# Gate and up products of a feed-forward layer: one weight sum made by an accumulating transfer, casts and loads in a new order, fifth and sixth product wide in 17 blocks

## The chip, the cores and the metric

The kernel runs on one core of one Trainium2 chip. The metric is the device time of one execution in microseconds (us). A core has TensorE (PE in the profile; PEld are its weight loads), VectorE (DVE), ScalarE (ACT), GpSimd (POOL) and SyncE (SP). SP and POOL issue the transfers of this kernel; 16 DMA engines of the core carry them all.

## The reference

One decoder layer over 512 tokens of width 1024 in float32: a mixer (stick-breaking attention beside a gated short convolution), a cross-attention into 256 memory tokens, and a SwiGLU feed-forward block, each with an RMS norm ahead and a residual add behind. The change lies in the first half of the feed-forward block:

```python
hf = rms_norm(x, norm_ffn[l])
gate, up = jnp.split(hf @ w_ffn_in[l], 2, axis=-1)      # 1024 x (2 * 2816)
x = x + (jax.nn.silu(gate) * up) @ w_ffn_out[l]
```

## The kernel before, in words

**Blocks and products.** The 2816 hidden channels are worked off in 22 blocks of 128 (`NF`, block number `m`). For one block the weights form a 2 x 2 scheme (gate or up, even or odd 128-row part of the 1024 inputs), and so do the activations (tokens 0 to 255 or 256 to 511, even or odd part). The kernel uses the seven-product form of a 2 x 2 matrix product: products `i` = 0 to 6, each of 128 channels by 256 tokens, summed over `KP` = 4 pairs of parts. "Fifth and sixth product" are `i` = 4 and 5. Products 0, 3, 4 and 5 go to the PSUM bank `z` of the block, 1 to `v`, 2 and 6 to `y` ("zvyzzzy"). Products 3, 4 and 5 are added onto what stands in `z`, so ACT or DVE read `z` between them; likewise product 6 is added onto product 2 in `y`.

**High and low parts.** Every operand is split into a rounded high part (float32r, cast by ACT) and a low part (the difference, by DVE). A product is high times high, high times low and low times high. *Narrow*, this is three matmuls of 256 columns for each k, twelve in all. *Wide*, the two halves of the activation lie side by side, so one matmul of 512 columns does the first two terms into the two halves of the bank, and one of 256 columns does the third: eight in all. A wide product leaves a second half in the bank that must be added. Before the change products 1, 2 and 6 are wide in all blocks, 5 in the 14 blocks of `WIDE` (5 to 18), and 0, 3 and 4 in none.

**Weight forms.** `ffn_load(m)` fetches for each block: `wg` (two parts as they are: products 0 and 1), and `ws`, one part loaded twice by SP, onto which POOL issues an accumulating transfer of two further parts (products 4 and 2). `sum_third` (DVE) adds a part of `ws` onto the first half of `wg`: product 3. `load_corner` fetches one more part into the tile `w2` (rows `a`; product 5), and `sum_last` (DVE) writes the sum of the two halves of `wg` beside it: product 6. Each pair is then cast by ACT and its low part taken by DVE: cast A (`pair_cast(m, 0)`, from `wg`), B (`pair_cast(m, 1)`, from `ws`), C (`pair_cast(m, 2)`, from the corner tile), and T (`third_cast(m)`, one half). "Rest A" and so on below are the DVE subtractions behind these casts (`rest_of`; line 1006 in the profile).

**What sets the order.** PE, ACT and DVE run an order written out by hand: the list `uses` names products in turn, in the middle of the stage (m,3), (m,2), (m,4), (m+1,0), (m+1,1), (m,5), (m,6) and so on; behind each product stands what reads it (`reads`), and then what `at` and `made` hang on that place (`made` puts the cast there and the rest one or two places later). Here and below (m,i) is product i of block m. SP and POOL are ordered by the framework: a transfer waits for its own data and for its buffer, and for what stands ahead of it in its queue. `wr` has four buffers and `wg` of `fpool` two: together the `ws` and `wg` of three blocks.

**Evictions.** `second(m)` joins product 2 in `y` with what ACT copied out of `z` after product 4; `evict(m, 0..2)` scales, applies SiLU (ACT) and multiplies; in `WIDE` blocks `evict(m, 2)` first adds the two halves of `z`.

Of the kernel before, what the change touches and what calls it, by code (L numbers as in the profile page):

```python
# [8 lines left out]
F32 = mybir.dt.float32  # L9
F32R = mybir.dt.float32r  # L10
AF = mybir.ActivationFunctionType
ALU = mybir.AluOpType
# [32 lines left out]
def hybrid_layer(ctx: ExitStack, tc: tile.TileContext, xT_d, memT_d, mem_d, cols_d, wv_d, win_d,  # L45
# [18 lines left out]
    def nm(s):  # L64
        count[0] += 1
        return f"{s}{count[0]}"
# [40 lines left out]
    def after(i, earlier):  # L107
        for e in earlier:
            tc.add_manual_dep(i.ins, e.ins.name, mybir.DependencyInfo(
                mybir.DependencyClass.NoSync, mybir.DependencyReason.DATA), reason="order")  # L110
# [588 lines left out]
    def forms_of(xe, xo):  # L699

        b11, b12, b21, b22 = xe[:, :HS], xe[:, HS:], xo[:, :HS], xo[:, HS:]
        c, d = f(unit("c1")), f(unit("c2"))
        n1, t3, n2, t4 = c[:, :HS], c[:, HS:], d[:, :HS], d[:, HS:]
        nc.vector.tensor_tensor(out=n1, in0=b11, in1=b12, op=ALU.subtract)
        nc.vector.tensor_tensor(out=t3, in0=b22, in1=b12, op=ALU.subtract)
        nc.vector.scalar_tensor_tensor(out=n2, in0=n1, scalar=-1.0, in1=b22, op0=ALU.mult,  # L708
                                       op1=ALU.subtract)
        nc.vector.scalar_tensor_tensor(out=t4, in0=n2, scalar=-1.0, in1=b21, op0=ALU.mult,  # L710
                                       op1=ALU.subtract)
        u = unit("xf")
        nc.scalar.copy(u[:, :HS], b11)
        nc.vector.tensor_tensor(out=u[:, HS:], in0=b11, in1=f(u[:, :HS]), op=ALU.subtract)
        a, b = slice(0, HS), slice(HS, S)

        def beside(src, s):
            both = unit(s)
            nc.scalar.copy(both[:, a], src)
            nc.vector.tensor_tensor(out=both[:, b], in0=src, in1=f(both[:, a]), op=ALU.subtract)  # L720
            return both[:, a], both[:, b], both

        first = beside(b21, "xo")
        second, fourth = beside(n1, "xc"), beside(t3, "xc")
        third, fifth = beside(n2, "xd"), beside(t4, "xd")
        last = beside(b22, "xo")
        return [(u[:, a], u[:, b]), first, second, third[:2], fourth[:2], fifth, last]

    def residual(w_dram, act, old, gain, pairs=False):

# [112 lines left out]

    KP = KD // 2
    raws, corners = {}, {}

    def ffn_load(m):

        a = wfi_d[m].rearrange("p (i c) -> p i c", i=4)
        s13, wg = ((fpool, "wg") if (m % 3, t) in ((1, "ws"), (2, "wg")) else (wpool, "wr")  # L850
                   for t in ("ws", "wg"))
        s13 = s13[0].tile([P, 2, 512], F32, tag=s13[1], name=nm("ws"))
        i = nc.sync.dma_start(s13, a[:, 2:3, :].broadcast_to([P, 2, 512]))
        if m < 2:
            after(i, [loads[-6]])
        wg = wg[0].tile([P, 2, 512], F32, tag=wg[1], name=nm("wg"))
        i = nc.sync.dma_start(wg, a[:, 0:2, :])
        if m < 2:
            after(i, [loads[-6]])
        if m < 2:  # L860
            load_corner(m)
        nc.gpsimd.dma_start(s13, a[:, 0:4:3, :], accum_op=ALU.add)  # L862
        raws[m] = wg, s13

    def load_corner(m):

        a22 = corners[m] = fpool.tile([P, 2, 512], F32, tag="w2", name=nm("a22"))
        i = nc.sync.dma_start(a22[:, 0, :], wfi_d[m][:, 3 * 512:])
        if m < 2:
            after(i, [loads[-6]])  # L870
# [4 lines left out]

    def sum_last(m, eng=nc.vector):
        wg = raws[m][0]
        eng.tensor_tensor(out=corners[m][:, 1, :], in0=wg[:, 0, :], in1=wg[:, 1, :], op=ALU.add)

    wforms = {}  # L880

    def pair_cast(m, which):

        raw = (*raws[m], corners[m])[which]
        hi = wpool.tile([P, 2, 512], F32R, tag="wh", name=nm("wf"))
        lo = wpool.tile([P, 2, 512], F32R, tag="wl", name=nm("wf"))
        nc.scalar.copy(hi, raw)
        for n, i in enumerate(((0, 1), (4, 2), (5, 6))[which]):
            wforms[m, i] = hi[:, n, :], lo[:, n, :]
        return raw, hi, lo  # L890
# [11 lines left out]
    def product(ps, m, i, ks=range(KP)):  # L902

        rests = []
        for k in ks:
            hi, lo = (w[:, k * P:(k + 1) * P] for w in wforms[m, i])
            xh, xl, *both = x2f[k][i]
            if both and (i != 5 or m in WIDE):
                nc.tensor.matmul(ps, hi, both[0], start=i < 3 and k == 0, stop=False,  # L909
                                 skip_group_check=True)  # L910
                rests.append((ps[:, :HS], lo, xh))
                continue
            for j, (a, b) in enumerate(((hi, xh), (hi, xl), (lo, xh))):
                nc.tensor.matmul(ps[:, :HS], a, b, start=i < 3 and k == 0 and j == 0,  # L914
                                 stop=k == KP - 1 and j == 2, skip_group_check=True)
        for operands in rests:
            nc.tensor.matmul(*operands, start=False,  # L917
                             stop=ks[-1] == KP - 1 and operands is rests[-1],
                             skip_group_check=True)

    WIDE = range(5, NF - 3)
    banks, silus = {}, []
    acts = {}

# [10 lines left out]
    def joined_halves(out_, bank, old):  # L935
        nc.vector.tensor_tensor(out=out_, in0=bank[:, :HS], in1=old, op=ALU.add)
        nc.vector.tensor_tensor(out=out_, in0=bank[:, HS:], in1=out_, op=ALU.add)

    def reads(m, i):

        b = banks[m]
        z, s, t = b["z"][:, :HS], b["s"], b["t"]
        if i == 5 and m in WIDE:
            nc.scalar.copy(s[:, :HS], b["z"][:, HS:])
        elif i in (0, 3, 4):
            nc.scalar.copy((s[:, :HS], None, None, s[:, HS:], t[:, :HS])[i], z)  # L946
        elif i == 1:
            joined_halves(b["g"][:, :HS], b["v"], s[:, :HS])
        elif i == 6:
            joined_halves(b["g"][:, HS:], b["y"], s[:, HS:])  # L950

    def second(m):
        b = banks[m]
        joined_halves(b["t"][:, HS:], b["y"], b["t"][:, :HS])

    def evict(m, part):
        b = banks[m]
        g = b["g"]
        if part == 0:
            nc.vector.tensor_tensor(out=g, in0=g, in1=r2b[0], op=ALU.mult)  # L960
        elif part == 1:
            silus.append(nc.scalar.activation(g, g, AF.Silu))
        else:
            j, odd = divmod(m, 2)
            if not odd:
                acts[j] = f(unit("a1")), f(unit("a2"))
            to = slice(odd * HS, (odd + 1) * HS)
            first = b["z"][:, :HS]
            if m in WIDE:
                first = b["s"][:, :HS]  # L970
                nc.vector.tensor_tensor(out=first, in0=b["z"][:, :HS], in1=first, op=ALU.add)
            for half, u in enumerate((first, b["t"][:, HS:])):
                sl = slice(half * HS, (half + 1) * HS)
                nc.vector.scalar_tensor_tensor(out=acts[j][half][:, to], in0=u, scalar=-1.0,
                                               in1=g[:, sl], op0=ALU.mult, op1=ALU.mult)
            if not odd:
                n1 = acts[j][1][:, :HS]
                nc.vector.tensor_tensor(out=n1, in0=acts[j][0][:, :HS], in1=n1, op=ALU.subtract)
# [140 lines left out]
    def at(n, *some):  # L1119
        todo.setdefault(n, []).extend(some)  # L1120
# [16 lines left out]
    at(14, lambda: evict(0, 1))  # L1137
    at(15, lambda: evict(0, 2))
    for m in range(NF - 2):
        at(uses.index((m, 1)), lambda m=m: ffn_load(m + 2))  # L1140
    for m in range(1, NF - 1):
        p = {i: uses.index((m, i)) for i in range(2, 7)}
        q = {i: uses.index((m + 1, i)) for i in range(2)}
        if m > 1:
            at(p[3], lambda m=m: sum_third(m + 1))
            at(p[3], lambda m=m: evict(m - 1, 0))
            at(p[2], lambda m=m: evict(m - 1, 1))
            at(q[0], lambda m=m: evict(m - 1, 2))
            made(p[3], pair_cast, m, 2)
            made(p[2], third_cast, m + 1)  # L1150
        else:
            made(p[4], third_cast, m + 1)
        at(p[4], lambda m=m: second(m))
        if m + 2 < NF:
            at(p[4], lambda m=m: load_corner(m + 2))
        made(q[0], pair_cast, m + 1, 1, late=2)
        at(q[1] if m < NF - 2 else p[4], lambda m=m: sum_last(m + 1))
        if m + 2 < NF:
            made(p[5], pair_cast, m + 2, 0)
    at(uses.index((0, 4)), lambda: second(0))  # L1160

# [373 lines left out]
```

## Time and profile before

| | |
|---|---|
| three runs | 839.65 us median (839.28 to 840.1) |
| the profiled execution | 838.75 us, of it a span of 837.0 us |
| granted TensorE clock | 0.998 |
| busy in the span | PE 828.8 us, DVE 684.6, ACT 463.9, POOL 161.2 |
| gate and up stage | from about 502.5 to 721.3 us of the span |
| in it, busy | PE 218.82 us of 218.82, DVE 210.82, ACT 121.81, POOL 24.83 |

The profile gives the span in microseconds from its start. A row of the chain or of the timeline starts with its start and its length; the length of a matmul in the timeline is its latency, so that neighbours overlap, and the time that a product takes is the distance from its start to the next one's. A group's row ends with its busy time, the mean length of one in ns, and the idle time of the engine just before its members. "x12" counts instructions.

### The profile page before, as it was taken

To read this page: it belongs to the slowest core of one execution; us is meant where nothing else is said; L and a number is where in the kernel's file an instruction comes from. 1 tells how busy PE (TensorE), PEld (TensorE's weight loads), DVE (VectorE), ACT (ScalarE), POOL (GpSimd) and SP (SyncE) were. 2 spreads that over 40 slices of the span, in tenths; PEclk is the share of its full clock that TensorE was granted. 3 is DMA by queue.
4 is the path that set the end of the run, shared out by engine and by line. 5 is a ranking of instruction groups with operands and counts; after the bars stand their busy time and mean duration, and the time that the engine had idled before them with its cause. 6 is when DMAs were issued, how large, how long until landed. Compare 5 with 4: busy or idle time off the path is not lost.

```text
span 837.0 us, 11962 instructions
## 1 busy us (share of the span) xinstructions
PE 828.8 (99%) x4374; PEld 714.1 (85%) x4374; DVE 684.6 (82%) x1086; ACT 463.9 (55%) x796; POOL 161.2 (19%) x168
## 2 busy tenths in 40 slices
PE   9999999999999999999999999999999999999996
PEld 7888888888888888888888789999999999888885
DVE  7879899996756576587555698999999999999886
ACT  7567868674332355434444566645555555576654
POOL 0011131110566630173000031111111110000401
PEclk9999999999999999999999999999999999999999
DMA  8552435235687865566431326677767673465552
GB/s 303 155 166 101 122 111 103 74 115 174 228 312 276 304 249 188 182 233 249 148 82 51 101 51 161 167 184 200 197 180 197 176 184 95 170 213 197 180 183 101
DMA packets 51357, 143.69 MB, mean 172 GB/s; under 512 B 5761, under 2 KB 7041, under 8 KB 48482
## 3 DMA queue, kind: packets, MB, share of 16 engines
q1 hardware_dynamic: 41650, 107.89, 38.2%
q0 software_dynamic: 9360, 34.75, 15.8%
q8 instruction: 34, 0.56, 0.3%
q10 hardware_dynamic: 288, 0.28, 0.1%
q14 instruction: 25, 0.20, 0.1%
HBM read 125.20 MB, written 13.64 MB: 166 GB/s over the span
## 4 chain that ended last, share of the span: by engine, by line
PE 99%; DVE 0%; ACT 0%; DVEq 0%; issue 0%
PE z L914 13%; PE p L1228 12%; PE pr L161 8%; PE pr L162 8%; PE pr L163 8%; PE y L909 5%; PE r L162 3%; PE r L163 3%; PE r L161 3%; PE v L288 3%; PE y L917 2%; PE v L909 2%; PE km L666 2%; PE mq L163 2%; PE mq L161 2%; PE mq L162 2%
## 5 line engine op out<-in xcount | busy, mean ns | idle before, releaser
L156 ACT CAST wh<-wr 128x1024 fp32r<-128x1024 f32 x84 | 88.0, 1051 | 144.2 <-issue 80.0
L157 DVE TENSOR_TENSOR wl<-wr,wh 128x1024 fp32r<-128x1024 f32 x84 | 111.0, 1321 | 32.0 <-ACT wh L156 31.9
L161 PE MATMUL pr<-xgh,wh 128*128 128x512 f32 x288 | 112.8, 392 | 0.0
L162 PE MATMUL pr<-xgl,wh 128*128 128x512 f32 x288 | 112.4, 390 | 0.0
L163 PE MATMUL pr<-xgh,wl 128*128 128x512 f32 x288 | 112.3, 390 | 0.0
L611 POOL TENSOR_TENSOR pre<-pre 128x512 f32<-128x512 f32 x44 | 70.9, 1616 | 31.5 <-DMA pre<-in_w_ffn_out_dram 29.2
L862 POOL DMA_DIRECT2D ws<-in_w_ffn_in_dram x22 | 26.6, 1209 | 248.5 <-DVE c L708 54.0
L163 PEld LDWEIGHTS pr<-xgh,wl 128*128 128x128 f32 x288 | 54.1, 188 | 11.5
L161 PEld LDWEIGHTS pr<-xgh,wh 128*128 128x128 f32 x288 | 54.1, 188 | 10.6
L162 PEld LDWEIGHTS pr<-xgl,wh 128*128 128x128 f32 x288 | 54.1, 188 | 10.5
L914 PE MATMUL z<-xd,wf 128*128 128x256 f32 x360 | 47.5, 282 | 0.0
L946 ACT COPY sa<-z 128x256 f32<-128x256 f32 x44 | 16.4, 373 | 51.9 <-PE z L914 51.9
L914 PEld LDWEIGHTS z<-xd,wf 128*128 128x128 f32 x360 | 45.0, 190 | 0.1
L1006 DVE TENSOR_TENSOR wf<-wg,wf 128x1024 fp32r<-128x1024 f32 (+1 forms) x44 | 43.1, 978 | 1.5
L1006 DVE TENSOR_TENSOR wl<-wr,wh 128x1024 fp32r<-128x1024 f32 x33 | 41.0, 1242 | 1.8 <-ACT wh L1073 1.8
L1073 ACT CAST wh<-wr 128x1024 fp32r<-128x1024 f32 x33 | 34.5, 1050 | 5.3 <-ACT f01h L1002 2.6
L914 PE MATMUL z<-xf,wf 128*128 128x256 f32 x264 | 35.4, 283 | 0.0
L914 PE MATMUL z<-xc,wf 128*128 128x256 f32 x264 | 35.1, 283 | 0.0
L914 PEld LDWEIGHTS z<-xf,wf 128*128 128x128 f32 x264 | 33.4, 192 | 0.1
L914 PEld LDWEIGHTS z<-xc,wf 128*128 128x128 f32 x264 | 33.0, 190 | 0.0
L368 DVE TENSOR_TENSOR g<-pr,r0b 128x512 f32<-128x512 f32 x16 | 11.0, 687 | 23.5 <-PE pr L163 23.5
L417 POOL TENSOR_SCALAR_AFFINE_SELECT e<-e 128x128 f32<-128x128 f32 (+1 forms) x24 | 10.7, 447 | 86.6 <-DVE e L470 86.6
(356 smaller groups left out, 2239.9 us busy)
## 6 DMA issues: line engine op xcount, KB each, us to landing
wr<-in_w_in_dram SPq DMA_DIRECT2D x36, 512.0 KB, 3.4
pre<-in_w_ffn_out_dram POOLq DMA_DIRECT2D x11, 1024.0 KB, 8.0
sums<-pre POOLq DMA_DIRECT2D x11, 1024.0 KB, 5.0
ws<-in_w_ffn_in_dram SPq DMA_DIRECT2D x22, 512.0 KB, 4.8
wg<-in_w_ffn_in_dram SPq DMA_DIRECT2D x22, 512.0 KB, 4.7
ws<-in_w_ffn_in_dram POOLq DMA_DIRECT2D x22, 512.0 KB, 5.7
wr<-sums SPq DMA_DIRECT2D x22, 512.0 KB, 4.0
wr<-in_w_ffn_out_dram SPq DMA_DIRECT2D x16, 512.0 KB, 3.7
```

What stands on the lines that cost most here:

```text
L156: after(nc.scalar.copy(h2, raw), lead[-1:])
L157: lows.append(nc.vector.tensor_tensor(out=l2, in0=raw, in1=f(h2), op=ALU.subtract))
L161: nc.tensor.matmul(ps, a[0], b[0], start=start, stop=False, **kw)
L162: nc.tensor.matmul(ps, a[0], b[1], start=False, stop=False, **kw)
L163: nc.tensor.matmul(ps, a[1], b[0], start=False, stop=stop, **kw)
L611: nc.gpsimd.tensor_tensor(out=t[:, a, :], in0=t[:, a, :], in1=t[:, b, :], op=ALU.add)
L862: nc.gpsimd.dma_start(s13, a[:, 0:4:3, :], accum_op=ALU.add)
L909: nc.tensor.matmul(ps, hi, both[0], start=i < 3 and k == 0, stop=False, skip_group_check=True)
L914: nc.tensor.matmul(ps[:, :HS], a, b, start=i < 3 and k == 0 and j == 0, stop=k == KP - 1 and j == 2, skip_group_check=True)
L1006: nc.vector.tensor_tensor(out=lo, in0=src, in1=f(hi), op=ALU.subtract)
L1073: nc.scalar.copy(hi, raw)
L1228: nc.tensor.matmul(res[i][s2], a[:, ts], b, start=j == 0 and n == 0, stop=n == 2 and j == (BEHIND - 1 if (i, s2) == (5, 1) else NJ - 1))
```

## The change

1. Product 4 becomes wide in the blocks of `WIDE`, as product 5 already is, and `WIDE` becomes blocks 3 to 19 (17 blocks, before 5 to 18). So 17 products 4 and three products 5 (blocks 3, 4, 19) become wide. In these blocks ACT copies both halves of `z` after product 4 (512 columns, before 256), and `second` becomes `folded`: one DVE add of 512 columns, one of 256 (before two of 256).
2. In blocks 4 to 20 (`OWN`) `sum_last` is no DVE add: POOL issues a transfer that accumulates the first half of `wg` onto its second half, within SBUF. The corner part is then loaded over the first half of `wg`, and cast C reads `wg`. The tile `w2` is left for blocks 0 to 3 and 21.
3. For these blocks the order changes: `ws` is loaded earlier in the program than `wg` from block 6 on, cast A stands one product earlier, `sum_third` stands directly behind rest A (two products earlier), cast T one product earlier ahead of cast C, and the corner load three products later by the program.

DVE, from rest C of block 7 on (the low part of its corner pair). Before:

```order
L1006 TENSOR_TENSOR wf1139_5661<-a221108_5464,wf1138_5660 128x1024
L1006 TENSOR_TENSOR wf1141_5674<-wg1119_5504,wf1141_5674 128x512
L936 TENSOR_TENSOR sb1129_5583<-y1140_5663,sb1129_5583 128x256
L937 TENSOR_TENSOR sb1129_5583<-y1140_5663,sb1129_5583 128x256
L971 TENSOR_TENSOR sa1110_5467<-z1109_5466,sa1110_5467 128x256
L974 SCALAR_TENSOR_TENSOR a11146_5710<-sa1110_5467,fg1117_5491 128x256
L974 SCALAR_TENSOR_TENSOR a21147_5711<-sb1111_5468,fg1117_5491 128x256
L978 TENSOR_TENSOR a21147_5711<-a11146_5710,a21147_5711 128x256
L936 TENSOR_TENSOR fg1151_5720<-v1150_5719,sa1144_5695 128x256
L937 TENSOR_TENSOR fg1151_5720<-v1150_5719,fg1151_5720 128x256
L878 TENSOR_TENSOR a221126_5579<-wg1119_5504 128x512
L1006 TENSOR_TENSOR wf1149_5717<-ws1118_5502,wf1148_5716 128x1024
```

And now, from the same rest C:

```order
L1028 TENSOR_TENSOR wf1136_5641<-wg1098_5374,wf1135_5640 128x1024
L968 TENSOR_TENSOR sb1125_5561<-y1137_5643,sb1125_5561 128x512
L969 TENSOR_TENSOR sb1125_5561<-sb1125_5561 128x256
L993 TENSOR_TENSOR sb1108_5450<-z1106_5448,sb1108_5450 128x256
L996 SCALAR_TENSOR_TENSOR a11141_5683<-sb1108_5450,fg1114_5474 128x256
L996 SCALAR_TENSOR_TENSOR a21142_5684<-sb1108_5450,fg1114_5474 128x256
L1000 TENSOR_TENSOR a21142_5684<-a11141_5683,a21142_5684 128x256
L949 TENSOR_TENSOR fg1146_5693<-v1145_5692,sa1139_5668 128x256
L950 TENSOR_TENSOR fg1146_5693<-v1145_5692,fg1146_5693 128x256
L1028 TENSOR_TENSOR wf1144_5690<-ws1101_5415,wf1143_5689 128x1024
L1028 TENSOR_TENSOR wf1149_5707<-wg1130_5593,wf1148_5706 128x1024
L884 TENSOR_TENSOR wg1130_5593<-ws1118_5526,wg1130_5593 128x512
```

The last add of the sum pair (L878) is gone, the join of product 2 is a wide and a narrow add (L968, L969), rest T now stands ahead of rest C and so is not in this piece, and rest A and `sum_third` (L884) of the block after next follow rest B at once.

POOL in the middle of the stage. Before:

```order
L862 DMA ws1118_5502<-in_w_ffn_in_dram 128x2x512
L862 DMA ws1134_5615<-in_w_ffn_in_dram 128x2x512
L862 DMA ws1152_5731<-in_w_ffn_in_dram 128x2x512
L862 DMA ws1168_5844<-in_w_ffn_in_dram 128x2x512
L862 DMA ws1186_5960<-in_w_ffn_in_dram 128x2x512
```

And now:

```order
L870 DMA ws1101_5415<-in_w_ffn_in_dram 128x2x512
L889 DMA wg1098_5374<-wg1098_5374 128x512
L870 DMA ws1118_5526<-in_w_ffn_in_dram 128x2x512
L889 DMA wg1115_5485<-wg1115_5485 128x512
L870 DMA ws1133_5634<-in_w_ffn_in_dram 128x2x512
L889 DMA wg1130_5593<-wg1130_5593 128x512
```

Between two accumulating loads of `ws` stands the new transfer (L889) of the block before.

SP in the same place (`a22` are corner tiles). Before:

```order
L857 DMA wg1119_5504<-in_w_ffn_in_dram 128x1024
L853 DMA ws1118_5502<-in_w_ffn_in_dram 128x2x512
L868 DMA a221108_5464<-in_w_ffn_in_dram 128x512
L853 DMA ws1134_5615<-in_w_ffn_in_dram 128x2x512
L857 DMA wg1135_5617<-in_w_ffn_in_dram 128x1024
L868 DMA a221126_5579<-in_w_ffn_in_dram 128x512
```

And now:

```order
L857 DMA ws1118_5526<-in_w_ffn_in_dram 128x2x512
L875 DMA wg1098_5374<-in_w_ffn_in_dram 128x512
L863 DMA wg1130_5593<-in_w_ffn_in_dram 128x1024
L857 DMA ws1133_5634<-in_w_ffn_in_dram 128x2x512
L875 DMA wg1115_5485<-in_w_ffn_in_dram 128x512
L863 DMA wg1147_5704<-in_w_ffn_in_dram 128x1024
```

The corner load (L875) goes into the `wg` whose sum was just made, and the load of the `wg` two blocks on stands right behind it.

The diff, cut:

```diff
-        return [(u[:, a], u[:, b]), first, second, third[:2], fourth[:2], fifth, last]
+        return [(u[:, a], u[:, b]), first, second, third[:2], fourth, fifth, last]
...
+    OWN = range(4, NF - 1)
+    own_sums = []
+    def ffn_load(m, which=("s", "g")):
...
+        if "s" in which:
+            after(nc.gpsimd.dma_start(s13, a[:, 0:4:3, :], accum_op=ALU.add), own_sums[-1:])
     def load_corner(m):
+        if m in OWN:
+            nc.sync.dma_start(raws[m][0][:, 0, :], wfi_d[m][:, 3 * 512:])
+            return
...
     def sum_last(m, eng=nc.vector):
         wg = raws[m][0]
+        if m in OWN:
+            own_sums.append(nc.gpsimd.dma_start(wg[:, 1, :], wg[:, 0, :], accum_op=ALU.add))
+            return
...
-            if both and (i != 5 or m in WIDE):
+            if both and (i not in (4, 5) or m in WIDE):
...
-    WIDE = range(5, NF - 3)
+    WIDE = range(3, NF - 2)
...
-        if i == 5 and m in WIDE:
-            nc.scalar.copy(s[:, :HS], b["z"][:, HS:])
+        if m in WIDE and i == 4:
+            nc.scalar.copy(t, b["z"])
+        elif m in WIDE and i == 5:
+            nc.scalar.copy(t[:, :HS], b["z"][:, HS:])
...
+    def folded(out_, bank, old):
+        nc.vector.tensor_tensor(out=old, in0=bank, in1=old, op=ALU.add)
+        nc.vector.tensor_tensor(out=out_, in0=old[:, :HS], in1=old[:, HS:], op=ALU.add)
     def second(m):
         b = banks[m]
+        if m in WIDE:
+            folded(b["t"][:, HS:], b["y"], b["t"])
+            return
...
-        at(uses.index((m, 1)), lambda m=m: ffn_load(m + 2))
+        if m + 2 in OWN and m > 3:
+            at(uses.index((m - 1, 3)), lambda m=m: ffn_load(m + 2, "s"))
+            at(uses.index((m, 1)), lambda m=m: ffn_load(m + 2, "g"))
+        else:
+            at(uses.index((m, 1)), lambda m=m: ffn_load(m + 2))
...
-            at(p[3], lambda m=m: sum_third(m + 1))
+            if m + 1 in OWN:
+                made(p[3], third_cast, m + 1)
+                at(p[2], lambda m=m: load_corner(m + 1))
+            else:
+                at(p[3], lambda m=m: sum_third(m + 1))
...
-        at(q[1] if m < NF - 2 else p[4], lambda m=m: sum_last(m + 1))
-        if m + 2 < NF:
+        if m + 1 not in OWN:
+            at(q[1] if m < NF - 2 else p[4], lambda m=m: sum_last(m + 1))
+        if m + 2 in OWN:
+            made(q[1], pair_cast, m + 2, 0)
+            at(p[5], lambda m=m: sum_third(m + 2), lambda m=m: sum_last(m + 2))
+        elif m + 2 < NF:
             made(p[5], pair_cast, m + 2, 0)
```

More of the change, by code (lines that the diff above doesn't have):

```diff
@@ L845, in hybrid_layer @@
     raws, corners = {}, {}
-    def ffn_load(m):
+    OWN = range(4, NF - 1)
+    own_sums = []
+    def ffn_load(m, which=("s", "g")):
         a = wfi_d[m].rearrange("p (i c) -> p i c", i=4)
@@ L851, in ffn_load @@
                    for t in ("ws", "wg"))
[L852 to L859, printed above, removed]
+        if "s" in which:
+            s13 = s13[0].tile([P, 2, 512], F32, tag=s13[1], name=nm("ws"))
+            i = nc.sync.dma_start(s13, a[:, 2:3, :].broadcast_to([P, 2, 512]))
+            if m < 2:
+                after(i, [loads[-6]])
+            raws[m] = None, s13
+        if "g" in which:
+            wg = wg[0].tile([P, 2, 512], F32, tag=wg[1], name=nm("wg"))
+            i = nc.sync.dma_start(wg, a[:, 0:2, :])
+            if m < 2:
+                after(i, [loads[-6]])
+            raws[m] = wg, raws[m][1]
         if m < 2:
             load_corner(m)
-        nc.gpsimd.dma_start(s13, a[:, 0:4:3, :], accum_op=ALU.add)
-        raws[m] = wg, s13
+        if "s" in which:
+            after(nc.gpsimd.dma_start(s13, a[:, 0:4:3, :], accum_op=ALU.add), own_sums[-1:])
     def load_corner(m):
+        if m in OWN:
+            nc.sync.dma_start(raws[m][0][:, 0, :], wfi_d[m][:, 3 * 512:])
+            return
         a22 = corners[m] = fpool.tile([P, 2, 512], F32, tag="w2", name=nm("a22"))
@@ L882, in pair_cast @@
     def pair_cast(m, which):
-        raw = (*raws[m], corners[m])[which]
+        raw = (*raws[m], raws[m][0] if m in OWN else corners[m])[which]
         hi = wpool.tile([P, 2, 512], F32R, tag="wh", name=nm("wf"))
@@ L969, in evict @@
             if m in WIDE:
-                first = b["s"][:, :HS]
+                first = b["t"][:, :HS]
                 nc.vector.tensor_tensor(out=first, in0=b["z"][:, :HS], in1=first, op=ALU.add)
@@ L1149, in hybrid_layer @@
             made(p[3], pair_cast, m, 2)
-            made(p[2], third_cast, m + 1)
+            if m + 1 not in OWN:
+                made(p[2], third_cast, m + 1)
         else:
@@ L1153, in hybrid_layer @@
         at(p[4], lambda m=m: second(m))
-        if m + 2 < NF:
+        if m + 2 < NF and m + 2 not in OWN:
             at(p[4], lambda m=m: load_corner(m + 2))
         made(q[0], pair_cast, m + 1, 1, late=2)
-        at(q[1] if m < NF - 2 else p[4], lambda m=m: sum_last(m + 1))
-        if m + 2 < NF:
+        if m + 1 not in OWN:
+            at(q[1] if m < NF - 2 else p[4], lambda m=m: sum_last(m + 1))
[3 more added lines that the diff above has]
+        elif m + 2 < NF:
             made(p[5], pair_cast, m + 2, 0)
```

## The prediction

> **What bounds the kernel now.** First the page: its span and busy time, and the chain that ended last.
>
> ```profile
> span 837.0 us, 11962 instructions
> PE 828.8 (99%) x4374; PEld 714.1 (85%) x4374; DVE 684.6 (82%) x1086; ACT 463.9 (55%) x796; POOL 161.2 (19%) x168
> PE 99%; DVE 0%; ACT 0%; DVEq 0%; issue 0%
> ```
>
> PE is the chain. The change lies in the gate and up stage, so I took that stage apart next: busy time of each engine in four blocks in which product 5 is narrow, and in thirteen in which it is wide.
>
> ```profile
> core 0: us, PE busy (x) PEld busy (x) DVE busy (x) ACT busy (x) POOL busy (x), PEclk, DMA share, GB/s
> 521.50:561.26 39.76, 39.76 (x290) 37.67 (x289) 38.67 (x67) 22.35 (x35) 4.79 (x5) 1.00 0.71 184
> 571.17:700.05 128.88, 128.88 (x886) 119.74 (x885) 124.89 (x215) 70.11 (x117) 15.65 (x13) 1.00 0.70 182
> ```
>
> PE has no gap in either stretch. DVE is close behind: 124.89 / 13 = 9.61 us of work in a block of 9.91. ACT and POOL are loosely filled, the transfers take 0.70 of the DMA engines' time. So a block lasts as long as its matmuls, and DVE would pace it if it got 0.3 us more work. The chain in order of time gives the length of a block, read between first matmuls of product 1 of successive blocks:
>
> ```profile
> 521.50 0.93 PE v L909 x4
> ...
> 561.26 0.93 PE v L909 x4
> ...
> 571.17 0.93 PE v L909 x4
> ...
> 582.49 0.93 PE z L909 x4
> 583.42 0.48 PE z L917 x4
> 583.89 0.93 PE y L909 x4
> 585.29 1.43 PE z L914 x12
> 586.73 0.93 PE y L909 x4
> ...
> 700.05 0.93 PE v L909 x4
> ```
>
> Four blocks with a narrow product 5: (561.26 - 521.50) / 4 = 9.940 us. Thirteen with a wide one: (700.05 - 571.17) / 13 = 9.914 us. One product made wide therefore gives back 0.026 us. The single products say the same, only coarser: wide 583.89 - 582.49 = 1.40 us, narrow 586.73 - 585.29 = 1.44 us.
>
> **The change part by part.**
>
> *The wide products.* Seventeen products 4 and three products 5 become wide: 20 x 0.026 = 0.53 us less on PE, which is the path. From the coarse rows the bounds are 20 x 0.02 = 0.4 and 20 x 0.04 = 0.8 us; I take 0.53, since it is the mean of many blocks. The Trainium skill's page "TensorE: Matmul & The Clock Gate", section Back-to-back issue gap, prices a matmul at its columns over 2.4 GHz plus about 2.5 ns; a wide product has four matmuls fewer, so by the page it saves 10 ns and the twenty 0.2 us. The trace disagrees with that size (26 ns), and its number stands.
>
> *DVE.* These rows price what is taken and added (mean ns behind the busy time):
>
> ```profile
> L878 DVE TENSOR_TENSOR a<-wg 128x512 f32<-128x512 f32 x20 | 13.6, 681 | 0.0
> L937 DVE TENSOR_TENSOR sb<-y,sb 128x256 f32<-128x256 f32 x22 | 9.3, 424 | 0.7
> L936 DVE TENSOR_TENSOR sb<-y,sb 128x256 f32<-128x256 f32 x22 | 9.2, 418 | 0.2 <-ACT sb L946 0.2
> L971 DVE TENSOR_TENSOR sa<-z,sa 128x256 f32<-128x256 f32 x14 | 5.8, 413 | 0.0
> L743 DVE TENSOR_TENSOR x<-r,x 128x512 f32<-128x512 f32 x1 | 0.7, 690 | 1.0 <-PE r L163 1.0
> ```
>
> Taken: 17 sums of 0.68 = 11.6 us. Added: 17 joins grow from 0.42 + 0.42 to 0.69 (the add that reads PSUM at 512 columns, L743) + 0.42, so 0.27 x 17 = 4.6 us, and three more adds of the `z` halves, 3 x 0.41 = 1.2 us. Net 5.8 us less on DVE, in a middle block 9.61 - 0.68 + 0.27 = 9.20 us. On the path this is nothing, because PE waits for DVE nowhere in the stage; it only widens a margin from 0.3 to 0.7 us a block. Block 3 goes the other way (wide, but its sum still on DVE), and `sum_third` of block 4 comes early: 0.27 + 0.69 = about 1.0 us more before the first relief, against 0.27 us of idle (39.76 - 38.67 over four). So DVE runs some 0.7 us late near 545 us. Next to be late there is rest B of block 4:
>
> ```profile
> 545.06 1.22 DVE L1006 TENSOR_TENSOR wf<-ws,wf 128x1024 fp32r<-128x1024 f32 x1
> 547.82 0.63 PE L917 MATMUL y<-xc,wf 128*128 128x256 f32 x4
> ```
>
> It ends at 546.28 and would end near 547.0; the first matmul that reads a low part there starts at 547.82. Cost nothing.
>
> *ACT.* Seventeen copies of 512 instead of 256 columns. Rows: 607 ns for a cast of 512, 364 for the copy of 256, so 0.24 us each, on an engine that is busy 70.11 of 128.88 us.
>
> ```profile
> L895 ACT CAST wf<-wg 128x512 fp32r<-128x512 f32 x21 | 12.8, 607 | 1.5 <-DVE wg L874 1.5
> L946 ACT COPY sb<-z 128x256 f32<-128x256 f32 x22 | 8.0, 364 | 3.2 <-PE z L914 3.1
> ```
>
> The join behind it starts 0.24 us later and is needed only by product 6, three products on. Nothing.
>
> *The accumulating transfer, and what waits for it.* No row shows a transfer within SBUF that adds. Nearest are POOL's loads of `ws`, which add too, and POOL's small transfers:
>
> ```profile
> ws<-in_w_ffn_in_dram SPq DMA_DIRECT2D x19, 512.0 KB, 4.8
> ws<-in_w_ffn_in_dram POOLq DMA_DIRECT2D x19, 512.0 KB, 5.7
> a<-in_w_ffn_in_dram SPq DMA_DIRECT2D x20, 256.0 KB, 2.8
> rt<-row POOLq DMA_DIRECT2D x1, 2.0 KB, 3.0
> q0 software_dynamic: 5232, 9.97, 27.4%
> ```
>
> The new one has half the bytes of a `ws` add, so it lands 3.0 to 5.7 us after its issue; I take the upper end, for it runs beside a `ws` load. Now a chain stands that was not there: `sum_third` on DVE, the transfer on POOL, the corner load on SP, cast C on ACT, rest C on DVE, product 5 on PE. For block 9 the old rows give the clock:
>
> ```profile
> 583.75 0.68 DVE L878 TENSOR_TENSOR a<-wg 128x512 f32<-128x512 f32 x1
> 584.35 1.22 DVE L1006 TENSOR_TENSOR wf<-ws,wf 128x1024 fp32r<-128x1024 f32 x1
> 586.27 1.21 DVE L1006 TENSOR_TENSOR wf<-wg,wf 128x1024 fp32r<-128x1024 f32 x1
> 587.52 0.69 DVE L874 TENSOR_TENSOR wg<-ws,wg 128x512 f32<-128x512 f32 x1
> 596.95 1.06 ACT L887 CAST wf<-a 128x1024 fp32r<-128x1024 f32 x1
> ```
>
> The sum at 583.75 goes, so rest B (1.22), rest A (1.21) and `sum_third` (0.69) run from 583.75 to about 586.9. Add 5.7: 592.6, the corner may be fetched. Add 0.3 for its issue and 2.8: 595.7. Cast C stands at 596.95, and 0.61 later now that cast T is ahead of it: 597.56. Margin 1.9 us. Queued behind the waiting instructions: on SP the load of `wg` of block 11, issued near 592.9 and needed about ten us later by cast A; on POOL the add onto `ws` of block 11, whose own load is still landing. Neither is late. POOL's issue (1.2 us a block) lies in idle time. The load itself: 19 `ws` adds took 27.4% of a window of 222 us, 3.2 us of all engines each; half of that, 1.6 us, lifts the DMA share from 0.70 to 0.86. The Trainium skill's page "DMA: Bandwidth & Descriptors", section Anatomy of one DMA, has about 2.0 us plus bytes over 436 GB/s for a transfer from POOL, here 2.6 us, which would leave a margin of 5 us; the `ws` row (5.7, by the page 3.2) says this is too short.
>
> *Sum.* 838.75 - 0.53 = 838.22 us for the profiled execution; that execution lies 0.90 us under the median of the three runs, so the median falls to 839.65 - 0.53 = **839.1 us**. What a measurement here can tell from no change is about 0.2%, 1.7 us; this gain is 0.06%.
>
> **The rivals.**
>
> *Slower: the corner comes late.* Landings spread, as these rows say of the `ws` and of the corner transfers (second from the tile `ws`, first from `a`):
>
> ```profile
> DMA to landing us min/median/max: 2.4/2.5/5.1
> DMA to landing us min/median/max: 3.9/5.5/8.3
> ```
>
> If add and corner together take longer than the margin allows, DVE stands at rest C with everything behind it, `sum_third` of the next block too, and the wait feeds itself. From rest C of a block to the end of `sum_third` two blocks on DVE has, by the rows, 1.22 + 1.11 + 0.41 + 0.84 + 0.21 + 0.84 + 2.43 + 0.69 = 7.75 us of work; with 0.3 for the issue and 1.06 for the cast, two blocks can't be shorter than 9.1 us plus the two landings. Two blocks of PE are 19.8, so it decides from 10.7 us on, against 8.5 from the medians. At the two maxima (13.4) each block grows by 1.35 us, 17 x 1.35 = 23 us, 862 us; halfway (12.0) by 0.65, 11 us, 850 us. For it: the DMA share rises to 0.86. Against: both transfers must be slow in most blocks, and the medians leave 2.2 us. Chance 0.09.
>
> *Slower: the DMA engines become the bound.* If the new transfer takes the engines as long as a `ws` add with double the bytes (3.2 us), the share is 1.02 and a block lasts 10.1 us: 17 x 0.2 = 3.4 us, less the 0.5, 842.5 us. Against: packets and bytes are half. Chance 0.04.
>
> *No gain.* The wide product 4 saves nothing, since its place differs (its neighbours are narrow products 0 and wide 2): 839.4 to 839.7 us. For it: the difference is only a fiftieth of a product. Against: product 5 has the same shape. Chance 0.13; it lies within no change, as the forecast does. The 0.2 us of the Trainium skill's matmul rule above would give 839.45 us, inside this case.
>
> *Faster.* If DVE, not the array, set the pace of the matmuls, the 0.41 us taken from it would shorten 14 blocks: 5.7 us, 833.4 us. For it: DVE is busy 97% there. Against: PE shows no gap, and a narrow product lasts 1.43 us wherever DVE stands. Chance 0.04.
>
> That the change does not do what it says I leave out: the order shows the sums on POOL and the wide matmuls where they should be.
>
> **How the numbers follow.** Forecast 0.70, no gain 0.13, both inside 0.2%: same 0.83. Slower 0.09 + 0.04 = 0.13, faster 0.04. The forecast's own range is 838.4 to 839.9 us (the bounds of the first term, and the spread of the three runs about their median). The range of 8 in 10 adds the beginning of the late corner, some waits in a few blocks without the loop: 838.2 to 841.0 us.
>
> **What would show it.** Right: blocks of 9.89 us between first matmuls of product 1 in the middle of the stage (9.914 - 0.026), still no idle time of PE there; DVE busy near 9.2 us a block; ACT starting cast C straight behind cast T; the new transfer landing within 5.7 us. Wrong: DVE or ACT idle ahead of rest C or cast C with the corner load as what ended it, SP standing at the corner load for the transfer until past cast C's place, PE gaps at product 5, or a DMA share near 1. A faster block than 9.85 us would mean that PE was paced by something that the profile does not show.

## The result: 843.93 us, slower by 0.5%

| | before | after |
|---|---|---|
| median of six runs | 839.52 us (839.28 to 840.1) | 843.93 us (843.54 to 846.31) |
| ratio | 1 | 1.0060 (95%: 1.0046 to 1.0074); of the two medians alone 1.0053 |
| profiled execution, span | 838.75, 837.0 us | 846.11, 844.1 us |
| stage from product 1 of block 2 to the first matmul behind it | 199.82 us | 206.56 us |

The forecast was 839.1 us, with 0.83 on no change: wrong. Its sign went to the rival that had been given 0.09, and that rival's mechanism was only the neighbour of the one that acted. The profiled execution is one of the two longest of the six (846.11 and 846.31; the others took 843.54 to 843.97), so the losses read from it below are larger than those of the median.

The page of the kernel after: span, busy time, the chain that ended last.

```profile
span 844.1 us, 11820 instructions
PE 831.8 (99%) x4294; PEld 712.3 (84%) x4294; DVE 681.0 (81%) x1072; ACT 468.9 (56%) x799; POOL 175.4 (21%) x185
PE 92%; DVE 4%; DMA 2%; ACT 1%; issue 1%; DVEq 0%; ACTq 0%; SPq 0%
```

Before, PE alone was 99% of the chain. Now 7% of it runs through DVE, the transfers and ACT. Where that happens is seen in the chain in order of time; these are first matmuls of product 1 (tile `v`), and the piece that leads to the largest gap. (A row of DMA or "issue" is time in which the chain waited for a transfer, or for nothing that the profile shows.)

```profile
521.74 0.93 PE v L922 x4
...
541.59 0.93 PE v L922 x4
...
620.69 0.93 PE v L922 x4
...
677.35 0.69 DVE wg L884
678.34 5.41 DMA wg<-in_w_ffn_in_dram
683.97 0.83 issue
684.80 0.62 ACT fg L984
685.42 0.48 ACT sb L957
685.95 2.07 PE z L922 x4
...
697.17 0.93 PE v L922 x4
...
728.30 6.85 PE p L1263 x30
```

From 541.59 to 620.69 lie eight blocks without a gap: 9.888 us each, which is the 9.89 of the prediction. From 620.69 to 697.17 lie seven, 76.48 us, where 7 x 9.888 = 69.21 were due: 7.27 us are lost there, and nowhere else in the stage. The idle times say who was late (the number in brackets), first on PE, then on ACT.

```profile
642.12 1.20 PE L922 MATMUL z<-xd,wf 128*128 128x512 f32 x4 [0.27 <-ACT sb L957]
685.95 2.07 PE L922 MATMUL z<-xd,wf 128*128 128x512 f32 x4 [3.75 <-ACT sb L957]
```

```profile
683.85 1.04 ACT L900 CAST wf<-wg 128x1024 fp32r<-128x1024 f32 x1 [5.09 <-DMA wg<-in_w_ffn_in_dram]
```

Cast C (L900) waits 5.09 us for the corner load; rest C on DVE behind it; and on ACT, in order behind the cast and one activation, the copy of `z` (L957), for which product 5 waits on PE. That gap of 3.75 us costs more than its length, as the windows behind it show (columns: length, busy time of PE, PEld, DVE, ACT, POOL, granted clock, DMA share, GB/s).

```profile
541.59:620.69 79.10, 79.10 (x514) 72.04 (x513) 75.82 (x126) 44.91 (x72) 16.86 (x16) 1.00 0.83 200
685.90:688.00 2.10, 2.05 (x5) 1.67 (x6) 2.03 (x6) 2.10 (x3) 0.00 (x0) 0.50 0.43 148
688.00:691.40 3.40, 3.40 (x14) 3.01 (x13) 3.33 (x7) 0.43 (x2) 1.20 (x1) 0.50 1.00 255
691.40:694.00 2.60, 2.60 (x20) 2.43 (x19) 2.50 (x5) 1.04 (x3) 0.86 (x1) 0.99 1.08 265
```

For 5.5 us behind the gap the granted clock is 0.50, so 2.7 us more go. 0.27 + 3.75 + 2.7 = 6.7 of the 7.27 us; the remainder I did not follow.

**Why the corner is late there, and not at 560.** "Own sum" is the new accumulating transfer (L889) that makes the sum of a block in `OWN`. SP's own rows, then POOL's. On SP, L875 is the corner load (issued as soon as the own sum has landed), L863 the load of `wg` two blocks on and L857 the load of a `ws`. On POOL, L870 is the `ws` add and L889 the own sum. Ahead of them stands what SP waited for at the corner load: in total, times, longest.

```profile
SPq L875 <- DMA wg<-wg: 131.2, 17, 10.7
```

```profile
552.10 0.33 SPq L875 DMA_DIRECT2D wg<-in_w_ffn_in_dram  x1
...
572.31 0.33 SPq L875 DMA_DIRECT2D wg<-in_w_ffn_in_dram  x1
...
593.05 0.33 SPq L875 DMA_DIRECT2D wg<-in_w_ffn_in_dram  x1
593.48 0.37 SPq L863 DMA_DIRECT2D wg<-in_w_ffn_in_dram  x1
594.58 0.38 SPq L857 DMA_DIRECT2D ws<-in_w_ffn_in_dram  x1
...
613.52 0.33 SPq L875 DMA_DIRECT2D wg<-in_w_ffn_in_dram  x1
```

```profile
581.76 1.20 POOL L870 DMA_DIRECT2D ws<-in_w_ffn_in_dram  x1 [3.66 <-DMA ws<-in_w_ffn_in_dram]
587.45 0.90 POOL L889 DMA_DIRECT2D wg<-wg  x1 [4.48 <-DVE fg L949]
...
602.38 1.20 POOL L870 DMA_DIRECT2D ws<-in_w_ffn_in_dram  x1 [4.51 <-DMA ws<-in_w_ffn_in_dram]
607.22 0.90 POOL L889 DMA_DIRECT2D wg<-wg  x1 [3.63 <-DVE fg L949]
```

Follow one trip. The corner load is issued at 593.05, the load of `wg` right behind it and that of `ws` 1.5 us after it; POOL gets to its `ws` add when that `ws` has landed, at 602.38 (9.3 us for 256 + 512 + 512 KB on one queue). The own sum of 607.22 stands behind that add in POOL's queue, and its landing lets SP go at 613.52, 11.1 us after the `ws` add. So from a corner load to the one two blocks later it takes 20.5 us (613.52 - 593.05; the trip before, 593.05 - 572.31, 20.7; the mean of three from 552.10 is 20.47), where two blocks of PE take 19.78. Each block the corner is fetched some 0.35 us later against the block: 0.6 us behind product 1 at 552.10, 2.7 us at 613.52 (610.80 in the chain), until the margin ahead of cast C is gone. The own sums themselves are issued without drift (587.45 to 607.22 is 19.77), and so are the `ws` loads (574.80 to 594.58 is 19.78). What drifts is when they land: the lateness goes from the corner load to `ws` behind it in SP's queue, and from the `ws` add to the own sum behind it in POOL's.

The transfers' landings in the stage, and the own sum's spread:

```profile
ws<-in_w_ffn_in_dram POOLq DMA_DIRECT2D x19, 512.0 KB, 7.6
wg<-wg POOLq DMA_DIRECT2D x17, 256.0 KB, 6.0
wg<-in_w_ffn_in_dram SPq DMA_DIRECT2D x17, 256.0 KB, 3.6
q0 software_dynamic: 7680, 14.42, 37.1%
```

```profile
DMA to landing us min/median/max: 3.5/6.0/8.9
```

### The profile page after: what moved, and what is told of

Read it like the earlier page. It is cut to its first block, busy times and chain, and to the rows that moved or that the text cites. A ratio compares the mean times of both kernels' runs of the same rounds, so it can differ in the third digit from the quotient of the medians.

```text
span 844.1 us, 11820 instructions
## 1 busy us (share of the span) xinstructions
PE 831.8 (99%) x4294; PEld 712.3 (84%) x4294; DVE 681.0 (81%) x1072; ACT 468.9 (56%) x799; POOL 175.4 (21%) x185
## 4 chain that ended last, share of the span: by engine, by line
PE 92%; DVE 4%; DMA 2%; ACT 1%; issue 1%; DVEq 0%; ACTq 0%; SPq 0%
PE p L1263 12%; PE pr L161 8%; PE pr L162 8%; PE pr L163 8%; PE z L927 7%; PE y L922 4%; PE r L162 3%; PE r L163 3%; PE r L161 3%; PE z L922 3%; PE v L288 3%; PE y L930 2%; PE v L922 2%; PE km L666 2%; PE mq L163 2%; PE mq L161 2%
## 5 line engine op out<-in xcount | busy, mean ns | idle before, releaser
L1028 DVE TENSOR_TENSOR wf<-wg,wf 128x1024 fp32r<-128x1024 f32 (+1 forms) x61 | 63.1, 1046 | 9.4 <-ACT wf L900 8.8
L870 POOL DMA_DIRECT2D ws<-in_w_ffn_in_dram x22 | 26.6, 1210 | 188.2 <-DMA ws<-in_w_ffn_in_dram 82.0
L900 ACT CAST wf<-wg 128x1024 fp32r<-128x1024 f32 x39 | 41.0, 1051 | 12.4 <-DMA wg<-in_w_ffn_in_dram 10.6
L927 PE MATMUL z<-xd,wf 128*128 128x256 f32 x324 | 42.8, 283 | 0.0
L927 PEld LDWEIGHTS z<-xd,wf 128*128 128x128 f32 x324 | 40.7, 191 | 0.1
L889 POOL DMA_DIRECT2D wg<-wg x17 | 15.9, 934 | 61.9 <-DVE fg L949 44.5
```

What stands on the lines that cost most here:

```text
L1028: nc.vector.tensor_tensor(out=lo, in0=src, in1=f(hi), op=ALU.subtract)
```

## The experiments

My theory behind the result: a loop through two queues, corner load, `ws` load behind it on SP, `ws` add, own sum behind it on POOL, corner load. Rivals: the own sums' traffic as such (DMA engines 0.83 full), the new order of casts and loads, the wide products.

**Parts of the change.** Three kernels, each with a part of it.

Wide products alone, in the kernel before:

```diff
-            if both and (i != 5 or m in WIDE):
+            if both and (i not in (4, 5) or m in WIDE):
...
-    WIDE = range(5, NF - 3)
+    WIDE = range(3, NF - 2)
```

> The kernel before, with the wide products of the change alone: product 4 wide and WIDE 3 to 19; sums on VectorE and the old order of casts and loads. If the loss comes from the transfers (both transfer theories below), this one has no late corner: PE saves 20 x 0.026 = 0.5 us, and VectorE has 9.61 + 0.27 = 9.88 us of work in a block of 9.89, so it may fall behind a little: 839.0 to 841.0 us. If the wide products themselves cost the time, about 843 to 844 us.

Measured 842.5 us (842.14 to 842.88) against 839.33, ratio 1.0037 (1.0024 to 1.0051). That is above the 839.0 to 841.0 us that I expected if only the transfers were to blame, and below the 843 to 844 of the other case. The chain of this kernel runs through DVE (its shares by engine on the page, then two rows of it, a window, and the idle time of the weight loads):

```profile
PE 75%; DVE 18%; issue 3%; ACT 3%; DVEq 0%; ACTq 0%
```

```profile
562.41 0.61 DVE sb L955
...
703.82 0.61 DVE sb L955
```

```profile
562.19:703.82 141.63, 141.63 (x905) 126.94 (x904) 137.95 (x233) 77.21 (x128) 16.86 (x14) 1.00 0.70 179
```

```profile
PEld y L917 <- DVE wf L1015: 3.6, 7, 1.2
```

From the join (L955) at 562.41 to the same one fourteen blocks later at 703.82 it takes 141.41 us: 10.10 us a block, paced by DVE, whose busy time is 137.95 / 14 = 9.85 us. By busy time PE looks full still; its weight loads wait 3.6 us in all for low parts. Above the block of after that is 17 x 0.21 = 3.6 us, less the 0.5 of the wide products 3.1, as measured. So the wide products do need DVE relieved. In the changed kernel, where it is, blocks last 9.888 us until the corner is late, so this is not its loss. My estimate of DVE's margin in the kernel before: if the 0.25 us that stay empty even here (10.10 - 9.85) stay empty there too, they and 9.61 us of busy time make 9.86 of the 9.914, a margin of 0.05 us, not 0.3.

The own sums and their order, products as before:

```diff
-            if both and (i not in (4, 5) or m in WIDE):
+            if both and (i != 5 or m in WIDE):
...
-    WIDE = range(3, NF - 2)
+    WIDE = range(5, NF - 3)
...
-        if m in WIDE:
-            folded(b["t"][:, HS:], b["y"], b["t"])
-            return
```

> The changed kernel with the products as before (product 4 narrow, product 5 wide in 5 to 18): the sums by transfer and the new order alone. Theory of the loop of queues (add onto ws, then the own sum behind it on POOL, then the corner load that waits for it on SP, then the loads of wg and ws behind that, then the next add onto ws: 20.4 us for two blocks of 19.8): the corner comes later by 0.3 us a block and the stage stalls after about ten blocks: 842 to 847 us. Theory that the transfers are simply too many for the DMA engines: the same. If the wide products were to blame: 839.5 us.

Measured 846.88 us (841.32 to 847.64), ratio 1.0073 (1.0047 to 1.0099). The corner loads drift here too (552.40, 572.71, 593.77, 617.23: 20.3, 21.1, 23.5 us for two blocks), and PE waits twice:

```profile
625.04 1.20 PE L922 MATMUL z<-xd,wf 128*128 128x512 f32 x4 [1.95 <-ACT sb L959]
668.16 1.95 PE L922 MATMUL z<-xd,wf 128*128 128x512 f32 x4 [3.19 <-ACT sb L959]
```

The loss needs no wide product 4.

The same order, but the sum on DVE in the place where the transfer was issued:

```diff
-            own_sums.append(nc.gpsimd.dma_start(wg[:, 1, :], wg[:, 0, :], accum_op=ALU.add))
+            nc.vector.tensor_tensor(out=wg[:, 1, :], in0=wg[:, 0, :], in1=wg[:, 1, :], op=ALU.add)
```

> As the run with the sums alone, but each sum of blocks 4 to 20 made by VectorE in the same place of the order (onto the second half of wg), and the corner still loaded over the first half of wg: the new order without the transfer. Both transfer theories: no stall, 839.2 to 840.0 us, the add onto ws and the corner landing as early in the last block as in the fifth. If the new order of casts and loads is to blame by itself: 842 us or more.

Measured 839.4 us (839.01 to 840.05), ratio 1.0002 (0.9992 to 1.0011). Neither the order of casts and loads nor the corner's place in `wg` costs anything. What is left is the transfer: its traffic, or its place in the queues.

**Traffic without waiters.** The kernel before, with seventeen transfers of the same size and kind at the same places of POOL's queue. They add a part of `wg` onto a tile that nothing reads, so the output doesn't depend on them:

```diff
+        if 4 <= m < NF - 1:
+            idle[m] = nc.gpsimd.dma_start(spare, wg[:, 0, :], accum_op=ALU.add)
```

> The kernel before, with 17 more transfers on POOL that add the first half of wg of blocks 4 to 20 onto a tile that nobody reads, each between two adds onto ws as in the changed kernel. The same traffic, and nothing waits for it. Theory of the loop: no link from the extra transfer to the corner load, so no drift: 839.3 to 840.2 us, though landings are longer. Theory of too many transfers: every landing longer, the loads late, 842 to 845 us.

Measured 839.61 us (839.04 to 840.16), ratio 1.0002 (0.9992 to 1.0011). First a window of thirteen of its blocks, then the landing of the new transfers (the median, at the end):

```profile
571.47:700.34 128.87, 128.87 (x885) 119.74 (x885) 124.87 (x215) 70.11 (x117) 27.44 (x26) 1.00 0.87 210
```

```profile
spare<-wg POOLq DMA_DIRECT2D x17, 256.0 KB, 3.9
```

The DMA share is 0.87, above that of after, and a block still lasts 128.87 / 13 = 9.913 us. The traffic by itself costs nothing. Of long landings this run shows little: here the extra transfers are issued 5.6 to 9.1 us behind the `ws` add ahead of them, as the first own sums of the changed kernel are, and land in 3.9 us in the median.

**Cutting the loop in three places.** Each keeps wide products and own sums, and takes one link away or shortens it. First the link from own sum to corner load: the corner is fetched early, together with the second half of `wg`, into the tile `w2`, and the own sum adds the first half there. SP then hardly waits for an own sum (four times in the stage, 1.6 us in all, against the 131.2 us above); the price is 256 KB more to load per block.

```diff
-            nc.sync.dma_start(raws[m][0][:, 0, :], wfi_d[m][:, 3 * 512:])
+            t = corners[m] = fpool.tile([P, 2, 512], F32, tag="w2", name=nm("a22"))
+            lined(nc.sync.dma_start(t, wfi_d[m].rearrange("p (i c) -> p i c", i=4)[:, 1:4:2, :]))
...
-            own_sums.append(nc.gpsimd.dma_start(wg[:, 1, :], wg[:, 0, :], accum_op=ALU.add))
+            own_sums.append(nc.gpsimd.dma_start(corners[m][:, 0, :], wg[:, 0, :], accum_op=ALU.add))
```

> The changed kernel, wide products and sums by transfer, but the corner part and the second half of the sum are loaded beforehand into the tile w2 (one load of 512 KB in place of 256), and POOL adds the first half of wg onto them there: no load waits for the own sum, and SP runs ws, w2, wg in this order. More bytes than in the changed kernel, but the link from the own sum to the loads behind the corner is cut. Theory of the loop of queues: no drift, no stall, and the 0.5 us of the wide products show: 838.5 to 839.5 us. Theory of too many transfers: worse than the changed kernel, over 844 us.

Measured 839.95 us (839.13 to 840.2) against 839.47, ratio 1.0003 (0.9994 to 1.0011): no stall, though the median lies above my 838.5 to 839.5.

```profile
542.17:700.36 158.19, 158.19 (x1026) 144.06 (x1025) 151.21 (x250) 89.76 (x144) 33.76 (x32) 1.00 0.94 236
```

Sixteen blocks, 158.19 / 16 = 9.887 us, no gap, with the DMA engines 0.94 full. That excludes the traffic a second time, at more of it.

Second, the link on SP: the load of the `wg` two blocks on goes ahead of the corner load instead of behind it.

```diff
+            after(i, [g_loads[m + 2]] if m + 2 in g_loads else [])
...
-            at(uses.index((m, 1)), lambda m=m: ffn_load(m + 2, "g"))
+            at(uses.index((m - 1, 4)), lambda m=m: ffn_load(m + 2, "g"))
...
-                at(p[2], lambda m=m: load_corner(m + 1))
+                at(p[4], lambda m=m: load_corner(m + 1))
```

> The changed kernel with one thing turned in SP's queue: the load of wg two blocks on stands ahead of the corner load that waits for the own sum, no longer behind it. The loop of queues still exists (own sum, corner, load of ws, add onto ws, own sum), but without the 512 KB of wg in it: by 9.4 us for 1.28 MB behind the corner, some 4 us shorter than 20.4 for two blocks, under 19.8. Theory of the loop: no drift, 838.5 to 840.0 us. If the chain from sum to corner to cast alone were too long (the rival as I predicted it), still 842 us or more.

Measured 839.64 us (839.03 to 840.64), ratio 0.9999 (0.9991 to 1.0008). The link is shorter by one transfer of 512 KB, not gone, and so this kernel is near the edge: cast C still waits, nine times, 10.0 us in all, and PE once, 0.2 us. Its corner loads fall behind product 1 and catch up again, by 3.5 us at most; in the changed kernel they fall 7.5 us behind.

```profile
ACT wf L904 <- DMA wg<-in_w_ffn_in_dram: 10.0, 9, 2.3
PE z L926 <- ACT sb L961: 0.2, 1, 0.2
```

Third, the link on POOL: the `ws` add of a block is issued behind the own sum of the block before, where it stood ahead of it. The own sum then stands behind an add that was issued nine microseconds earlier.

```diff
+    LATE = range(6, NF - 1)
...
+    def late_add(m):
+        a = wfi_d[m].rearrange("p (i c) -> p i c", i=4)
+        after(nc.gpsimd.dma_start(raws[m][1], a[:, 0:4:3, :], accum_op=ALU.add), own_sums[-1:])
...
             at(p[5], lambda m=m: sum_third(m + 2), lambda m=m: sum_last(m + 2))
+            if m + 3 in LATE:
+                at(p[5], lambda m=m: late_add(m + 3))
```

> Edit: as the changed kernel, but from block 6 on POOL issues the accumulating load of ws of a block behind the own sum of the block before (before: ahead of it), so that an own sum stands behind a ws add issued about 9 us earlier, not 6 to 3 us. If the loop of queues is the cause (an own sum lands about 11 us after the ws add ahead of it), it is cut here at a third place: own sums land 3.5 to 5 us after their issue all along, the corner loads stay 9.9 us apart, blocks last 9.89 us, and the time is 839 to 840 us. The price is a new tight place: ws add (0.9 + 7.6 us) and then sum_third of the next block (0.7) make 9.5 us with the issue against 9.89; if that decides, DVE waits at sum_third for the ws transfer, and the time lies between 840 and 843 us. If instead own sums land late because the DMA engines are 0.8 to 0.85 full, the order on POOL changes nothing: landings grow from 3.5 to 9 us again and the time is 843 to 846 us.

Measured 839.33 us (838.64 to 839.9) against 839.48, ratio 0.9998 (0.9989 to 1.0007). Its own sums' landings, then its chain:

```profile
DMA to landing us min/median/max: 3.3/3.8/4.6
```

```profile
521.84 0.93 PE v L927 x4
...
541.69 0.93 PE v L927 x4
...
699.87 0.93 PE v L927 x4
...
721.12 8.89 PE p L1270 x39
```

The same transfer that took up to 8.9 us now lands within 4.6 us, and the edit changes only the order of two rows on POOL. The long landing was time behind the `ws` add. The kernel after says the same: each of its 17 own sums lands behind the `ws` add ahead of it, 1.2 to 5.1 us later, even the one that was issued only 0.7 us after it (669.50 and 668.79). Blocks last 158.18 / 16 = 9.886 us. The feared new tight place is there, but small: by the groups of its stage `sum_third` waits 1.3 us in all for the `ws` transfer.

**Fewer blocks.** If the lateness grows by 0.35 us a block, eight own sums should end before it reaches PE:

```diff
-    OWN = range(4, NF - 1)
+    OWN = range(4, 12)
...
-    FOURTH, WIDE = range(3, 11), range(3, NF - 3)
```

(The second line stands for product 4 wide in blocks 3 to 10, product 5 in 3 to 18.)

> The changed kernel with own sums in blocks 4 to 11 only and product 4 wide in blocks 3 to 10 (product 5 wide in 3 to 18). The same loop, in the same links, but for eight blocks. Theory of the loop with a drift of 0.3 us a block and a margin of two to three: it ends before the margin is used up, no stall, and ten products more are wide than before: 839.0 to 839.6 us. If every block lost a share at once, half of the loss of the changed kernel, 841 to 842 us.

Measured 839.68 us, but spread from 838.57 to 843.02 over eleven runs: six at 838.57 to 839.68, five at 840.38 to 843.02. The profiled one, 843.02, waits near the end of the eight, and has half the clock behind it (a row of idle times, then a window):

```profile
614.63 1.19 PE L922 MATMUL z<-xd,wf 128*128 128x512 f32 x4 [1.91 <-ACT sb L957]
```

```profile
617.00:619.00 2.00, 2.00 (x9) 1.71 (x8) 1.91 (x4) 0.93 (x1) 1.20 (x1) 0.50 0.44 148
```

My expectation fails as it stood: the lateness is not a steady ramp with a sure start, and eight blocks are enough in some executions. What sets the start was not followed further.

**No version beats the kernel before by what can be measured.** By the stage alone the predicted gain is there: from product 1 of block 2 to the first matmul behind the stage the kernel before takes 199.82 us (721.32 - 521.50), the one with POOL's order turned 721.12 - 521.84 = 199.28. That is 0.54 us less, read from one execution of each; over the whole program it is less than the spread of single runs.

```profile
721.32 8.89 PE p L1228 x39
```

## Why the prediction was wrong

- **The wide products: right.** Predicted 0.53 us off PE and blocks of 9.89 us; measured 9.888 and, in the stage without a stall, 0.54 us.
- **The accumulating transfer's landing: the failed step.** It took 5.7 us as an upper end from the median of the `ws` adds, added the corner's 2.8 and found a margin of 1.9 us for block 9. For that block the sum was about right: its corner load was issued at 593.05, by the prediction it "may be fetched" from 592.6 on. The fault is that the step was done for one block, as if the next started afresh. The landing isn't a property of the transfer: 3.3 to 4.6 us where the `ws` add ahead is old, up to 8.9 where it is young. The Trainium skill's page "DMA: Bandwidth & Descriptors", section Two DMAs through the same engine are not ordered, says that within one queue of one DMA engine descriptors start in order. The run with POOL's order turned agrees, with 3.8 against 6.0 us in the median.
- **"Queued behind the waiting instructions": the sentence that held the answer.** It named the load of `wg` on SP and the add onto `ws` on POOL, and closed with "Neither is late". It asked whether they are late for their casts. It did not ask who waits for them next: that `ws` add stands ahead of the next own sum, and so the chain closes. Written down, the loop needs 9.3 + 11.1 us against 19.8 for two blocks. This is what the step put at nothing: 0.35 us a block, which adds up block by block.
- **The rival "the corner comes late": right in its place, wrong in its loop.** It foresaw cast C and rest C waiting with the corner as what ended it. Its law ran through DVE: two blocks at least 9.1 us plus both landings, and so a threshold of 10.7 us for the two. The medians of after are 6.0 + 3.6 = 9.6, below it, and by that law nothing should have begun. The loop that decided ran through the two queues and did not need slow transfers, only ordinary ones in a row. The price was overrated (23 or 11 us; it was 4.4 in the median and 7.3 in the profiled execution), because the lateness grows by 0.35 us a block and reaches PE only in the second half of the stage.
- **DMA load: right.** The own sums took (37.1% of 228 us - 27.4% of 222) / 17 = 1.4 us of all engines each, predicted 1.6; the share rose to 0.83, predicted 0.86, and cost nothing even at 0.94.
- **DVE: sign right, size off, and the margin misjudged.** Predicted 9.20 us of busy time a block, measured 75.82 / 8 = 9.48. The prediction subtracted mean lengths of single records, but neighbouring records overlap, and busy time counts the overlap once: in these windows the records add up to 10.38 us a block before and 10.09 after, against 9.61 and 9.48 of busy time. So 0.16 of the missing 0.28 us is overlap; part of the rest is the window, whose eight blocks hold nine joins. The margin of 0.3 us was taken as idle share, and the run with the wide products alone showed DVE pacing the block at 9.85 us of busy time already.
- **ACT's longer copies, POOL's issue time: nothing, as predicted.** The same holds for the new order of casts, by the run that kept only it.

## What to carry to other kernels

When a transfer gets a waiter, draw the loop: follow what stands behind the waiter on its queue, who waits for that, and on until a row repeats; then hold the sum of the loop against the blocks that it spans. Here a loop 3.5% too long did nothing for ten blocks and then stalled, so a check of one early block proves little. Price a transfer by what its own queue holds ahead of it; the order of two issues can be worth more than the bytes.

## What was not expected of the hardware

The granted clock fell to 0.50 for 5.5 us behind a PE gap of 3.75 us, so the stall cost some 1.7 times its length. In the run with only the own sums, a gap of 3.19 us was followed by 11 us at a mean of 0.85 (0.50 to 0.62 for the first four, then 1.00), one of 1.95 us by none of it:

```profile
625.04:636.30 11.26, 11.26 (x75) 10.37 (x76) 10.95 (x21) 7.35 (x12) 2.24 (x3) 1.00 0.83 209
668.16:679.50 11.34, 11.34 (x66) 10.32 (x67) 11.03 (x21) 6.31 (x11) 3.31 (x3) 0.85 0.75 182
```

The Trainium skill's page "TensorE: Matmul & The Clock Gate", section What's actually happening, has half clock after an idle window of about 3.4 us. The half clock agrees with the 0.50, the gap of 3.75 too. But 3.19 us sufficed, and in the kernel with eight own sums even 1.91 us (0.50 from 617 to 619), so the measurements here give no such bound; what tells 1.91 from 1.95 is open.
